# Steps of a weight transform called after two of three matmul groups of the output projection

## The chip, the cores and the metric

The kernel runs on one core of a Trainium2 chip. The metric is the device time of one launch in microseconds (us). TensorE (PE) multiplies and writes to PSUM; VectorE (DVE), ScalarE (ACT) and GpSimd (POOL) do the elementwise work, and POOL has no access to PSUM; SyncE (SP) issues all the transfers. Each engine takes its instructions from a queue of its own, in order.

## The reference

One layer of a decoder on 1024 prompt tokens and 8 x 4 sample tokens (1056 in all), model width 1024, feed-forward width 2816, in fp32:

```
m = mixer(x)                                   # HGRN2 heads and retention heads, gated and normalised
x = layer_norm(alpha * x + m @ w_out)          # "output projection", then the first norm
hidden = silu(x @ w_gate) * (x @ w_up)         # 22 blocks of 128 hidden features
x = layer_norm(alpha * x + hidden @ w_down)
```

It returns x and the states of the two kinds of heads.

## The kernel before

All activations are transposed: features on partitions, tokens on the free axis, in four quarters `q` of 264 tokens. Each fp32 factor is split into a high part (a cast on ACT, L214) and a low part (a subtraction on POOL or DVE, L215), and each product is three matmuls: high x high, high x low, low x high. A group of 8 factor blocks is thus 24 matmuls into one PSUM bank `pj`; there are four such banks.

The stages that matter here follow each other so. The **output projection**, `oproj(pr)` for `pr` = 0 and 1 (two quarters each): for each of 8 output blocks `m` and both quarters one group, 32 groups in all; L1112 adds the result to `Y` on DVE. Its weights come through `w_out(m)` as raw tiles `wr` and are split into `bh` and `bl` (L214 on ACT, L215 on POOL). Then the **first norm** of each quarter (`norm`): squares on ACT (L771) summed on DVE (L773), a column sum on TensorE (L756), `rstd` with three Newton steps on DVE (L761, L239 to L243), a matmul that spreads `rstd` over the tokens (L747), the scaling (L784 on DVE, L788 on ACT or L786 on DVE), and the split into `X`, whose low part is on POOL for six of eight blocks. Then the **plain products**, `gu`: for each quarter, gate and up of the hidden blocks 0 and 1, L250 from `X`, with L1004 on ACT and L1005 on DVE behind them. Then the **block products** (`unit`, L921), which compute the other 20 hidden blocks in pairs with seven products in place of eight; their weights are combined in `blocks` (L896 to L903 on POOL). At the end w_down is applied (L1166) in the same seven-product way.

For that last stage the combined blocks ("forms") of w_down are prepared early, by the generator `forms()`, and kept in DRAM (`wb`). It goes over the 11 pairs `p` of w_down's row blocks with three buffers in turn (tile `XC`, `p % 3`). Per pair: two loads of 512 KB (L1018); a row sum on DVE (L1033, the "reduce"); two operations on POOL (L1035, L1036) in the pair's first step; two more (L1040, L1041) in its second; and four stores of 256 KB (L1022). A load into a buffer waits until the stores from it have landed. All loads and stores are issued by SP, among the loads of weights (L223) and of `Y` (L1099) and the stores of hidden values (`hd`, L978).

```
        wf = forms()
            ...
            for p in range(3):
                load(p)
            yield
            for p in range(NPAIR):
                ...
                yield          # after store(p - 1), reduce, L1035, L1036
                ...
                yield          # after load(p + 2), L1040, L1041
            store(NPAIR - 1)
```

So `wf` has 24 steps: one for the first three pairs' loads, 22, and the last store. `next(wf, None)` takes one. Before, it stands in `oproj` behind each `m` (16 steps) and in the plain products behind each of 8 calls of `gu`. `combine(1)`, which needs the buffers' space, takes whatever is left. Other side work (the norms, `combine`, `total` with L800) is in a list of generators from which `tick` takes steps.

Where an instruction is written is not where it runs: the program is put in order per engine by a scheduler that works with its own estimates before the run. A step that is called sooner is thus placed sooner, and the rows around it are placed anew, on every engine.

Of the kernel before, what the change touches and what calls it, by code (L numbers as in the profile page):

```python
# [141 lines left out]
def body(tc, ctx, a):  # L142
# [11 lines left out]
    def pj():  # L154
        return psb["p"].tile([P, 512], F32, tag="pj", name="pj", bufs=psb["pj"])
# [89 lines left out]
    def group(out, ls, rs, rate):  # L245
        n = len(ls) * 3
        i = 0
        for (lh, ll), (rh, rl) in zip(ls, rs):
            for l, r in ((lh, rh), (lh, rl), (ll, rh)):
                PE.matmul(out, l, r, start=(i == 0), stop=(i == n - 1))  # L250
                i += 1
            if i == n // 2:
                tick(rate)
        tick(rate)

    def wk(w):
        return [(hi[:, k], lo[:, k]) for hi, lo in w for k in range(hi.shape[1])]

    def xk(c0, n):
        return [(X[:, 0, k, c0:c0 + n], X[:, 1, k, c0:c0 + n]) for k in range(KT)]  # L260


    with ExitStack() as ctxA:
# [450 lines left out]
        def w_out(m):  # L714
            wo[m] = load_w(wc[:, :, m * P:(m + 1) * P].rearrange("k p n -> p k n"))
# [6 lines left out]
    with ExitStack() as ctxB:  # L722
# [15 lines left out]
        def qs_(q):  # L738
            return slice(q * CQ, (q + 1) * CQ)
# [25 lines left out]
        def norm(q, g, b, w1=3, w2=3):  # L765
            n, sl = CQ, qs_(q)
            yield
            s2 = tt("s2")
            for m in range(KT):
                q2 = mx()[:, :n] if m else s2  # L770
                S.activation(q2, Y[:, m, sl], AF.Square)  # L771
                if m:
                    V.tensor_tensor(s2, s2, q2, op=add)  # L773
                if m % 2:
                    yield
            for _ in range(w1):
                yield
            rs = rstd([s2], n)
            for _ in range(w2):
                yield  # L780
            rb = spread(rs, n)
            for m in range(KT):
                y = Y[:, m, sl]
                V.tensor_tensor(y, y, rb, op=mul)  # L784
                if m in TA:
                    V.tensor_scalar(y, y, g[:, m:m + 1], b[:, m:m + 1], op0=mul, op1=add)  # L786
                else:
                    S.activation(y, y, AF.Identity, bias=b[:, m:m + 1], scale=g[:, m:m + 1])  # L788
                split(X[:, 0, m, sl], X[:, 1, m, sl], y, G if m in LG else V)
                if m % 2 and m < KT - 1:  # L790
                    yield
# [70 lines left out]
        def combine(pr):  # L862
            s0, s1 = qs_(2 * pr), qs_(2 * pr + 1)
            if pr:
                for _ in wf:
                    pass
                XB.append(pb.tile([P, 2, 3, HK, CQ], F32R, tag="XC", name="XC", bufs=1))
            yield
            for k in range(HK):
                t3, t2, t4 = [mx()[:, :CQ] for _ in range(3)]  # L870
                S.copy(t3, Y[:, HK + k, s1])
                V.tensor_tensor(t3, t3, Y[:, k, s1], op=sub)
                V.tensor_tensor(t2, t3, Y[:, k, s0], op=add)
                split(*btile("T3", pr, k), t3)
                yield
                V.tensor_tensor(t4, Y[:, HK + k, s0], t2, op=sub)
                split(*btile("T2", pr, k), t2)
                split(*btile("T4", pr, k), t4)
                yield
# [10 lines left out]
        def blocks(src, c, eng=None):  # L890
            E = eng or G
            w1, w2 = load_raw(src[c]), load_raw(src[c + 1])
            a11, a12, a21, a22 = w1[:, :HK], w1[:, HK:], w2[:, :HK], w2[:, HK:]
            out = {"A11": block(a11, eng)}
            f1 = pb.tile([P, HK, P], F32, tag="s1", name="s1", bufs=1)
            E.tensor_tensor(f1, a21, a22, op=add)  # L896
            E.tensor_tensor(a21, a11, a21, op=sub)
            E.tensor_tensor(a11, f1, a11, op=sub)  # L898
            out["S2"] = block(a11, eng)
            out["S3"] = block(a21, eng)  # L900
            out["S1"] = block(f1, eng)
            out["A12"] = block(a12, eng)
            E.tensor_tensor(a12, a12, a11, op=sub)  # L903
            out["A22"] = block(a22, eng)
            out["S4"] = block(a12, eng)
            return out
# [104 lines left out]
        def forms():  # L1011
            def raw(p):
                o = p % 3 * 2 * D
                return spare[:, o:o + 2 * D]

            def load(p):
                for i in range(2):
                    nc.sync.dma_start(raw(p)[:, i * D:i * D + D], a["w_down"][2 * p + i])  # L1018

            def store(p):  # L1020
                for n in range(4):
                    nc.sync.dma_start(wb[n, :, :, p, :].rearrange("m p n -> p m n"),  # L1022
                                      raw(p)[:, n * 512:n * 512 + 512].rearrange("p (m n) -> p m n", n=P))
# [5 lines that stand above are left out]
                a11, a21, a12, a22 = [raw(p)[:, n * 512:n * 512 + 512] for n in range(4)]  # L1029
                if p:  # L1030
                    store(p - 1)
                with behind(V):
                    V.tensor_reduce(rows[:, :2, p], raw(p).rearrange("p (i n) -> p i n", i=2), axis=AX, op=add)  # L1033
                with behind(G):
                    G.tensor_tensor(a11, a11, a21, op=sub)  # L1035
                    G.tensor_tensor(a21, a21, a22, op=add)  # L1036
                yield
                if p and p + 2 < NPAIR:
                    load(p + 2)
                G.tensor_tensor(a22, a22, a11, op=sub)  # L1040
                G.tensor_tensor(a12, a12, a22, op=sub)  # L1041
# [4 lines that stand above are left out]
# [47 lines left out]
                cnt["h"] += 1  # L1093
            return out

        cnt = {"w": 0, "h": 0}

        def xload(q, m):
            nc.sync.dma_start(Y[:, m, qs_(q)], xc[m, :, qs_(q)])  # L1099

        def oproj(pr):
            qs = (2 * pr, 2 * pr + 1)
            for i, m in enumerate(list(range(KT))[::1 - 2 * pr]):
                if m not in wo:
                    w_out(m)
                    wo.pop(m - 2 if pr == 0 else m + 2, None)
                for q in qs:
                    out = pj()[:, :CQ]
                    w, x = wk(wo[m]), xk(q * CQ, CQ)
                    group(out, [w[k] for k in GO], [x[k] for k in GO], RO)  # L1110
                    y = Y[:, m, qs_(q)]
                    V.scalar_tensor_tensor(y, y, ALPHA, out, op0=mul, op1=add)  # L1112
                    if pr == 0:
                        xload(q + 2, m)
                next(wf, None)
            for q in qs:
                side.append((("n1", q), norm(q, l1g, l1b)))
            side.append((("cb", pr), combine(pr)))
# [4 lines left out]
        for pr in range(2):  # L1123
            oproj(pr)

        h = {}
# [10 lines left out]
        for p in range(1, NPAIR):  # L1137
            h = {}
# [3 lines left out]
            w = blocks(a["w_gate"], 2 * p)  # L1142
# [91 lines left out]
def _program(ins):  # L1234
    import concourse.bacc as _bacc

    nc = _bacc.Bacc("TRN2", target_bir_lowering=False, num_devices=1, dynamic_dma_scratch_size=2048)
    a = {n: nc.dram_tensor(f"in_{n}", v.shape, mybir.dt.from_np(v.dtype), kind="ExternalInput").ap() for n, v in ins.items()}
    for n, s in _OUT.items():
        a["o_" + n] = nc.dram_tensor(f"out_{n}", s, F32, kind="ExternalOutput").ap()  # L1240
    a["st"] = [a["sh"], a["sr"]]
    a["so"] = [a["o_hp"], a["o_rp"]]
    a["sso"] = [a["o_hs"], a["o_rs"]]
    a["yT"] = a["o_yT"]
    with tile.TileContext(nc, schedule_with_timeline_sim=True) as tc, ExitStack() as ctx:
        body(tc, ctx, a)
    return nc
# [12 lines left out]
```

## Time and profile before

| | |
|---|---|
| time of the runs | 1316.63 us median of 3 (1314.59 to 1319.09) |
| profiled execution | 1313.48 us, span 1311.4 us |
| PE busy | 1285.0 us, 98% |
| DVE, ACT, POOL busy | 772.6, 506.9, 748.0 us |
| transfers | 170.50 MB, 130 GB/s over the span |
| output projection | from about 497 to 593 us |
| plain products | from about 593 to 648 us |
| block products, w_down | from 648 to 1060 us, to the end |

The times of all rows are from the start of the span. A row of an engine's timeline has the idle time ahead of it in brackets, and what ended it. "Busy" of PE counts matmuls that overlap, so that the number of matmuls in a stretch tells more than its busy time.

### The profile page before, as it was taken

How to read it: one execution, taken by the hardware profiler on the slowest of the kernel's cores; microseconds unless marked ns; L12 is line 12 of the kernel's file. 1: busy time of each engine (PE TensorE's matmuls, PEld its weight loads, DVE VectorE, ACT ScalarE, POOL GpSimd, SP SyncE). 2: the span in 40 equal slices, each digit the busy share in tenths (PEclk: the TensorE clock that was granted, in tenths of full speed). 3: DMA queues.
4: the chain of work that ended last, by engine and by line, in shares of the span. 5: the costliest groups of instructions: out<-in, count | busy, mean ns of one | idle time of the engine just before them, and what ended most of it. 6: DMA issues, size and time to landing. Idle time of an engine off the chain costs nothing.

```text
span 1311.4 us, 29620 instructions
## 1 busy us (share of the span) xinstructions
PE 1285.0 (98%) x11622; PEld 1259.1 (96%) x11622; DVE 772.6 (59%) x1675; ACT 506.9 (39%) x1120; POOL 748.0 (57%) x698
## 2 busy tenths in 40 slices
PE   9999999999999999999999999999999999999896
PEld 8999999999999999999899999999999999999896
DVE  7255443656575665489754654346544683777843
ACT  7243442232323233256542323323233354443552
POOL 2853331312122126798989888798786537675650
PEclk9999999999999999999999999999999999999898
DMA  8455312202111116987433323233232495656541
GB/s 287 141 174 187 134 35 83 69 16 80 55 65 52 50 51 212 300 244 237 138 94 102 123 91 102 75 102 119 94 103 70 145 304 163 180 180 180 156 135 67
DMA packets 156411, 170.50 MB, mean 130 GB/s; under 512 B 12272, under 2 KB 138864, under 8 KB 156272
## 3 DMA queue, kind: packets, MB, share of 16 engines
q1 hardware_dynamic: 156272, 168.62, 40.9%
q8 instruction: 91, 1.49, 0.5%
q14 instruction: 48, 0.39, 0.1%
HBM read 118.66 MB, written 49.91 MB: 129 GB/s over the span
## 4 chain that ended last, share of the span: by engine, by line
PE 91%; DVE 2%; POOL 2%; DMA 2%; issue 1%; ACT 1%; SPq 0%; ACTq 0%; POOLq 0%; DVEq 0%
PE pj L250 35%; PE mx L921 17%; PE pj L1166 16%; PE pj L921 14%; PE mx L482 1%; PE mx L625 1%; PE mx L595 1%; PE mx L627 1%; PE mx L250 1%; PE mx L577 1%; POOL X L215 1%; PE mx L666 1%; PE mx L537 1%; DMA XB<-hd 0%; DMA wr<-in_w_in 0%
## 5 line engine op out<-in xcount | busy, mean ns | idle before, releaser
L215 POOL TENSOR_TENSOR bl<-wr,bh 128x512 fp32r<-128x512 f32 x212 | 280.5, 1334 | 249.6 <-ACT bh L214 245.0
L250 PE MATMUL pj<-X,bh 128*128 128x352 f32 (+1 forms) x1888 | 417.9, 310 | 4.9 <-POOL X L215 3.3
L250 PEld LDWEIGHTS pj<-X,bh 128*128 128x128 f32 x1888 | 313.4, 189 | 9.6 <-POOL X L215 3.7
L250 PE MATMUL pj<-X,bl 128*128 128x352 f32 (+1 forms) x944 | 290.5, 308 | 0.1
L214 ACT CAST bh<-wr 128x512 fp32r<-128x512 f32 x220 | 133.0, 619 | 252.2 <-POOL wr L898 65.6
L250 PEld LDWEIGHTS pj<-X,bl 128*128 128x128 f32 x944 | 178.7, 189 | 0.8 <-DVE bl L215 0.4
L1166 PE MATMUL pj<-XC,X 128*128 128x264 f32 x858 | 149.1, 286 | 0.0
L1166 PE MATMUL pj<-XB,X 128*128 128x264 f32 x858 | 148.2, 285 | 0.0
L921 PE MATMUL pj<-X,bh 128*128 128x264 f32 x672 | 126.3, 287 | 0.4 <-DVE u L932 0.4
L1166 PEld LDWEIGHTS pj<-XC,X 128*128 128x128 f32 x858 | 123.1, 189 | 0.0
L1166 PEld LDWEIGHTS pj<-XB,X 128*128 128x128 f32 x858 | 122.6, 189 | 0.0
L921 PE MATMUL mx<-X,bh 128*128 128x264 f32 x608 | 112.4, 284 | 0.0
L921 PEld LDWEIGHTS pj<-X,bh 128*128 128x128 f32 x672 | 104.2, 188 | 0.9 <-DVE u L932 0.6
L1053 POOL TENSOR_TENSOR XC<-XC 128x264 fp32r<-128x264 f32 x71 | 67.0, 944 | 62.1 <-ACT XC L1052 62.0
L250 PE MATMUL pj<-bh,X 128*128 128x256 f32 x512 | 96.2, 285 | 0.0
L921 PE MATMUL pj<-X,bl 128*128 128x264 f32 x336 | 95.2, 284 | 0.0
L921 PEld LDWEIGHTS mx<-X,bh 128*128 128x128 f32 x608 | 93.8, 188 | 0.0
L1053 POOL TENSOR_TENSOR XB<-XB 128x264 fp32r<-128x264 f32 x71 | 68.9, 970 | 37.6 <-ACT XB L1052 32.6
L921 PE MATMUL mx<-X,bl 128*128 128x264 f32 x304 | 85.9, 282 | 0.0
L250 PEld LDWEIGHTS pj<-bh,X 128*128 128x128 f32 x512 | 79.9, 189 | 1.7 <-issue 1.0
L250 PE MATMUL pj<-bl,X 128*128 128x256 f32 x256 | 72.5, 283 | 0.0
L959 DVE TENSOR_TENSOR h<-mx,u 128x264 f32<-128x264 f32 x54 | 23.0, 431 | 69.0 <-PE mx L921 68.0
(260 smaller groups left out, 2659.2 us busy)
## 6 DMA issues: line engine op xcount, KB each, us to landing
hd<-h SPq DMA_DIRECT2D x154, 132.0 KB, 2.1
wr<-in_w_in SPq DMA_DIRECT2D x23, 512.0 KB, 3.7
XC<-in_w_down SPq DMA_DIRECT2D x22, 512.0 KB, 5.1
wb<-XC SPq DMA_DIRECT2D x44, 256.0 KB, 4.9
wr<-in_w_gate SPq DMA_DIRECT2D x22, 512.0 KB, 4.0
wr<-in_w_up SPq DMA_DIRECT2D x22, 512.0 KB, 3.6
XB<-hd SPq DMA_DIRECT2D x77, 132.0 KB, 3.2
XC<-hd SPq DMA_DIRECT2D x77, 132.0 KB, 3.4
```

The costliest lines, as they stand in the source:

```text
L214: S.copy(hi, src)
L215: (eng or V).tensor_tensor(lo, src, hi.bitcast(F32), op=sub)
L250: PE.matmul(out, l, r, start=(i == 0), stop=(i == n - 1))
L482: PE.matmul(into(B32 * b, (c % 4) * w), k[:, o:o + B32], cols(q, o), start=True, stop=True)
L537: PE.matmul(a_ps[:, c * C:(c + 1) * C], k[:, cc], q[:, cc], start=True, stop=True)
L577: PE.transpose(t_ps[:, c * C:(c + 1) * C], k[:, (4 * b + c) * C:(4 * b + c + 1) * C], ident)
L595: PE.matmul(d_ps[:, c * P:(c + 1) * P], tk[:, 4 * b + c], v[:, 4 * b + c], start=True, stop=True)
L625: PE.matmul(o[:, c * P:(c + 1) * P], at[:, cc], v[:, cc], start=True, stop=(cc == 0))
L921: PE.matmul(bank[pr], l[:, k], rs[k][r], start=(first and n == 0), stop=(n == 3 * HK - 1), skip_group_check=not first)
L959: V.tensor_tensor(g, ps, u, op=add)
L1053: eng.tensor_tensor(lo, raw, hi.bitcast(F32), op=sub)
L1166: PE.matmul(out, l, r, start=(i == 0), stop=(i == 3 * NPAIR - 1))
```

## The change

A counter of groups is kept in `cnt["g"]`, and `oproj` calls `next(wf, None)` inside the loop over the quarters, behind every group whose number is not a multiple of three: 22 calls in place of 16. The call behind each `gu` is not touched; it finds two steps left, where it found eight.

```
-        cnt = {"w": 0, "h": 0}
+        cnt = {"w": 0, "h": 0, "g": 0}
...
                     V.scalar_tensor_tensor(y, y, ALPHA, out, op0=mul, op1=add)
                     if pr == 0:
                         xload(q + 2, m)
-                next(wf, None)
+                    cnt["g"] += 1
+                    if cnt["g"] % 3:
+                        next(wf, None)
```

The scheduler's order moves with it (the changed file has two lines more, so lines from L1115 on are two higher there). First place: DVE, from the reduce that precedes quarter 2's `rstd`. `mx` is the tile with the variance, `XC` the buffers of the forms. Before (the reduce is pair 8's):

```order
L1005 TENSOR_TENSOR h<-pj,u 128x264
L1033 TENSOR_REDUCE rows<-XC 128x2
L761 TENSOR_SCALAR mx<-mx 128x3
L239 TENSOR_SCALAR ny_7641<-mx 128x3
L241 TENSOR_TENSOR mx<-mx,ny_7641 128x3
L242 SCALAR_TENSOR_TENSOR mx<-mx,ny_7641 128x3
```

Now (the reduces are those of pairs 9 and 10, and L1155 and L1156 are L1153 and L1154 of before):

```order
L1033 TENSOR_REDUCE rows<-XC 128x2
L773 TENSOR_TENSOR s_7587<-s_7587,mx 128x264 x2
L1033 TENSOR_REDUCE rows<-XC 128x2
L761 TENSOR_SCALAR mx<-mx 128x3
L1005 TENSOR_TENSOR h<-pj,u 128x264
L1155 TENSOR_SCALAR rows<-rows 128x22
L239 TENSOR_SCALAR ny_7670<-mx 128x3
L1156 TENSOR_TENSOR rows<-rows 128x11
L241 TENSOR_TENSOR mx<-mx,ny_7670 128x3
L242 SCALAR_TENSOR_TENSOR mx<-mx,ny_7670 128x3
L1005 TENSOR_TENSOR h<-pj,u 128x264
```

The last two reduces have moved from behind quarter 2's `rstd` to ahead of it. In the same way pair 5's reduce now stands ahead of quarter 0's L761, where pair 3's was the last before. On TensorE L747 of quarter 2 stands behind 1046 matmuls of 264 columns, before behind 1020.

Second place: POOL, from the first operation of `blocks` (L896) to the first X splits of quarter 2 (L215 with `X<-Y,X`). Before:

```order
L896 TENSOR_TENSOR s_8261<-wr 128x512
L1041 TENSOR_TENSOR XC<-XC 128x512
L1036 TENSOR_TENSOR XC<-XC 128x512
L897 TENSOR_TENSOR wr<-wr 128x512
L1040 TENSOR_TENSOR XC<-XC 128x512
L800 TENSOR_TENSOR s_8384<-Y 128x264
L1041 TENSOR_TENSOR XC<-XC 128x512
L800 TENSOR_TENSOR s_8384<-s_8384,Y 128x264 x6
L215 TENSOR_TENSOR X<-Y,X 128x264 x2
```

Now, the end of the same piece:

```order
L800 TENSOR_TENSOR s_8384<-s_8384,Y 128x264
L1040 TENSOR_TENSOR XC<-XC 128x512
L800 TENSOR_TENSOR s_8384<-s_8384,Y 128x264
L1041 TENSOR_TENSOR XC<-XC 128x512
L1035 TENSOR_TENSOR XC<-XC 128x512
L800 TENSOR_TENSOR s_8384<-s_8384,Y 128x264
L215 TENSOR_TENSOR X<-Y,X 128x264 x2
L1036 TENSOR_TENSOR XC<-XC 128x512
L800 TENSOR_TENSOR s_8384<-s_8384,Y 128x264
```

Counted over the queue since the output projection began, 32 operations of the forms stood ahead of these X splits before and 41 now, of `total` (L800) 7 before and 4 now; 12 of the forms stood behind them, now 3.

Third place: SP, from the first load of pair 9. Now:

```order
L1018 DMA XC<-in_w_down 128x1024
L223 DMA wr<-in_w_gate 128x1024
L1022 DMA wb<-XC 128x4x128
L1018 DMA XC<-in_w_down 128x1024
L1022 DMA wb<-XC 128x4x128 x2
L1018 DMA XC<-in_w_down 128x1024
L978 DMA hd<-h 128x264
L223 DMA wr<-in_w_gate 128x1024
L1022 DMA wb<-XC 128x4x128 x2
L1018 DMA XC<-in_w_down 128x1024
```

The loads (L1018) are pair 9's two and pair 10's two. Before, up to pair 9's second load:

```order
L223 DMA wr<-in_w_gate 128x1024
L1022 DMA wb<-XC 128x4x128
L223 DMA wr<-in_w_up 128x1024
L1022 DMA wb<-XC 128x4x128
L1018 DMA XC<-in_w_down 128x1024
L978 DMA hd<-h 128x264
L1022 DMA wb<-XC 128x4x128 x3
L1018 DMA XC<-in_w_down 128x1024
```

What moved is the weight load of `blocks` (the second L223 `in_w_gate`), from ahead of pair 9's first load to behind pair 10's first load.

## Rows read from the trace of the kernel before

**Rows 1.** The page's head: span, busy time by engine, TensorE's clock in tenths

```profile
span 1311.4 us, 29620 instructions
PE 1285.0 (98%) x11622; PEld 1259.1 (96%) x11622; DVE 772.6 (59%) x1675; ACT 506.9 (39%) x1120; POOL 748.0 (57%) x698
PEclk9999999999999999999999999999999999999898
```

**Rows 2.** Busy time by stretch, instructions in parentheses; then clock, DMA share, GB/s

```profile
506.00:560.00 54.00, 54.00 (x444) 53.84 (x444) 24.03 (x46) 13.18 (x28) 38.10 (x30) 1.00 1.00 309
560.00:600.00 40.00, 40.00 (x333) 40.00 (x332) 37.01 (x78) 26.66 (x64) 39.76 (x38) 1.00 0.76 226
600.00:610.00 10.00, 10.00 (x86) 10.00 (x84) 8.55 (x25) 4.49 (x14) 6.34 (x6) 1.00 0.95 299
610.00:620.00 10.00, 8.81 (x74) 8.60 (x72) 8.88 (x19) 7.63 (x20) 9.61 (x12) 1.00 0.83 258
630.00:640.00 10.00, 7.38 (x44) 6.74 (x43) 9.66 (x19) 6.81 (x18) 9.76 (x11) 0.83 0.50 145
```

**Rows 3.** What TensorE waited for, 560 to 860 us: total, times, longest

```profile
PE pj L250 <- POOL X L215: 3.3, 2, 2.1
PE pj L921 <- DVE u L932: 0.4, 1, 0.4
PE pj L250 <- DVE X L215: 0.3, 1, 0.3
PE pj L250 <- ACT X L214: 0.2, 1, 0.2
```

**Rows 4.** TensorE's timeline: start, us, then line, operation, count, idle time before

```profile
561.84 0.73 PE L747 MATMUL mx<-cst,rs 128*128 128x128 f32 x6
...
612.06 0.73 PE L747 MATMUL mx<-cst,rs 128*128 128x128 f32 x6
...
618.79 0.39 PE L250 MATMUL pj<-X,bh 128*128 128x264 f32 x1 [1.19 <-POOL X L215]
...
634.70 0.39 PE L250 MATMUL pj<-X,bh 128*128 128x264 f32 x1 [2.11 <-POOL X L215]
...
648.26 0.41 PE L921 MATMUL pj<-X,bh 128*128 128x264 f32 x2
```

**Rows 5.** POOL's timeline, same columns

```profile
551.16 1.30 POOL L1035 TENSOR_TENSOR XC<-XC 128x512 f32<-128x512 f32 x1 [4.01 <-DVE rows L1033]
...
592.41 2.55 POOL L215 TENSOR_TENSOR bl<-wr,bh 128x512 fp32r<-128x512 f32 x2
...
613.08 4.96 POOL L800 TENSOR_TENSOR s<-s,Y 128x264 f32<-128x264 f32 x6
617.99 1.47 POOL L215 TENSOR_TENSOR X<-Y,X 128x264 fp32r<-128x264 f32 x2
...
633.85 4.40 POOL L215 TENSOR_TENSOR X<-Y,X 128x264 fp32r<-128x264 f32 x6
```

**Rows 6.** What SP waited for, 500 to 660 us: total, times, longest

```profile
SPq L1018 <- DMA wb<-XC: 44.2, 11, 5.9
```

**Rows 7.** DVE's timeline: a reduce behind a load, then quarter 2's rstd

```profile
548.79 2.29 DVE L1033 TENSOR_REDUCE rows<-XC 128x2 f32<-128x2048 f32 x1 [5.11 <-DMA XC<-in_w_down]
...
606.93 0.16 DVE L761 TENSOR_SCALAR mx<-mx 128x3 f32<-128x3 f32 x1
609.01 0.42 DVE L773 TENSOR_TENSOR s<-s,mx 128x264 f32<-128x264 f32 x1
610.80 0.43 DVE L1005 TENSOR_TENSOR h<-pj,u 128x264 f32<-128x264 f32 x1 [1.37 <-PE pj L250]
...
641.14 0.17 DVE L1153 TENSOR_SCALAR rows<-rows 128x22 f32<-128x22 f32 x1
641.91 0.73 DVE L1154 TENSOR_TENSOR rows<-rows 128x11 f32<-128x11 f32 x1
```

**Rows 8.** SP's timeline: issues that follow each other

```profile
606.58 0.33 SPq L1018 DMA_DIRECT2D XC<-in_w_down  x1
607.00 0.38 SPq L978 DMA_DIRECT2D hd<-h  x1
```

**Rows 9.** Transfers issued in 600 to 620 us; landing times of all loads, all stores

```profile
wb<-XC SPq DMA_DIRECT2D x6, 256.0 KB, 4.6
XC<-in_w_down SPq DMA_DIRECT2D x3, 512.0 KB, 4.0
DMA to landing us min/median/max: 3.4/5.1/9.2
DMA to landing us min/median/max: 2.3/4.9/9.1
```

**Rows 10.** ACT's timeline: the cast of quarter 2's first X

```profile
614.83 0.40 ACT L214 CAST X<-Y 128x264 fp32r<-128x264 f32 x1
```

## The prediction

> **What bounds the kernel now.** I read the page's busy table and clock row first [rows 1]. TensorE is busy for 1285.0 of 1311.4 us and its clock is at its upper level, 2.4 GHz, nearly everywhere. So a gain can only come from a stretch in which TensorE loses time, and a loss from a new place where it has to wait.
>
> The table of stretches shows where that is [rows 2]. From 506 to 600 us (the output projection) TensorE has no idle time and issues 777 matmuls. From 600 on each 10 us should hold about 84; 610 to 620 holds 74, and 630 to 640 holds 44, with a granted clock of 0.83 (part of it at 1.2 GHz). In the same table POOL is busy 39.76 of 40 us from 560 to 600 and 9.6 us or more of 10 in four of the six stretches after it: there it is the full queue. The list of waits names the cause [rows 3]: `pj` waits for POOL's split of X twice, 3.3 us in all. The timeline places them: 1.19 us before 618.79, where quarter 2 of the plain products begins, and 2.11 us before 634.70 for quarter 3 [rows 4].
>
> The stretch thus loses 1.19 us at quarter 2; at quarter 3 it loses 2.11, 0.22 (ACT) and 0.29 (DVE) us of waits and, by the clock, (1 - 0.83) x 10 = 1.7 us. That is 5.5 us, the most that removing all of it could give.
>
> **The change part by part.** The forms need 24 calls of `next(wf)`: one for the first loads, two for each of the 11 pairs, one for the last store. Before, 16 came in the output projection. Now 22 of 32 groups make a call (every third none), so two remain, and the line beside the plain products, which is still there, takes them. Nothing is removed: 44 POOL operations, 11 reduces on DVE, 22 loads and 44 stores stay. What moves is their place in four queues, shown in the section on the change.
>
> *POOL.* Before quarter 2's first X split, POOL now runs 41 operations of the forms where it ran 32, and 4 additions of `total` (L800) where it ran 7; the 28 weight splits, the 12 earlier X splits and two of `blocks` are in both. A 128x512 operation takes 1.3 us in a row of its kind; an L800 4.96 / 6 = 0.83 us; an X split 4.40 / 6 = 0.73 us [rows 5]. That is 9 x 1.3 - 3 x 0.83 = 9.2 us more. Before, the split began at 617.99; with no idle time won back it begins at 627.2 and ends at about 628.0. POOL was idle for 54 - 38.10 = 15.9 us between 506 and 560 [rows 2], which could take up the extra work. But its gaps before the fourth pair are waits for loads (4.01 us before 551.16, behind the reduce), and the transfers were at a share of 1.00 there: they don't come sooner because steps are called sooner. On SP one more 256 KB store now stands ahead of that pair's second load, 0.85 us at 309 GB/s [rows 2], so I start the fourth pair at 552.0. I win back at most 2.3 us.
>
> *SP and DVE.* There are only three buffers. A pair's second load waits for the stores of the pair three before it, and this is SP's largest wait: 44.2 us in 11 times [rows 6]. A reduce then waits for the load, and everything on DVE waits behind it: before 548.79 DVE stood for 5.11 us in this way [rows 7]. There nobody needed DVE. Now the reduces of pairs 9 and 10 stand ahead of quarter 2's `rstd` (L761 and its Newton steps); before, only pair 8's did, and its load was there. The matmul that spreads `rstd` (L747) follows it, then the scaling, then the X splits; TensorE stands at L747 or, behind it, at the X split.
>
> The chain, from POOL's order: from pair 3's first operation to the last one of pair 6 there are 32 operations of 128x512 and 11 X splits, 32 x 1.3 + 11 x 0.73 = 49.6 us, ending at 601.6 if POOL doesn't idle. Then SP must see pair 6's last store land; issue pair 9's second load and two stores; wait for the second of these (pair 7's) before pair 10's first load; pass that, an `hd` store and a weight load; issue a store of pair 7, wait for it, and issue pair 10's second load. An issue takes about 0.45 us [rows 8]. In 600 to 620 us a store landed in 4.6 and a load in 4.0 us (medians); the shortest of all were 2.3 and 3.4 [rows 9]. With the medians: 601.6 + 4.6 + 0.9 + 4.6 + 1.4 + 4.6 + 4.0 = 621.7. The reduce takes 2.29, `rstd` 2.1 (606.93 to 609.01), two evictions of 0.43 and two operations on `rows` of 0.17 and 0.73 stand between [rows 7]: L747 can run at 627.9. From L747 (612.06) to the end of ACT's cast (614.83 + 0.40) and a POOL split of 0.73 it took 3.9 us [rows 4, 5, 10]: the first X is ready at 631.8. With the shortest landings it is 624.3.
>
> So two queues, worked out apart, give 628.0 (or 625.7 with idle time won back) and 624.3 to 631.8. **I take 628.0**, the sum that rests on POOL operations alone and lies in the middle of the other. By the order alone it can't be ready before 619.1: quarter 2's L747 now stands 26 matmuls later, 612.06 + 26 x 0.12 + 3.9 (0.12 us is 40.00 us for 333 matmuls [rows 2]).
>
> A rule of the Trainium skill speaks against so late a chain: "DMA: Bandwidth & Descriptors", section "Anatomy of one DMA", gives about 2.0 us fixed plus bytes at 436 GB/s, as an estimate 2.6 us for a store and 3.2 us for a load. If that chain alone decided, the first X would by it be ready at 625.0 and the change would cost 3.5 us, under the bound of 0.3%; the page measured the gpsimd path, and the medians here disagree with it, 4.6 and 4.0 us on a queue that is 83 to 95% busy.
>
> *From the first X of quarter 2 on.* Before, TensorE needed 648.26 - 618.79 = 29.5 us to the first block product (L921), of which 4.3 us are quarter 3's losses above; 25.1 us are left for 192 matmuls and quarter 3's small ones. After a wait of some 10 us the clock will fall as it did after the 2.11 us wait: 1.7 us. Quarter 3's X is no longer late: its six splits follow 10.8 us behind quarter 2's first (6 X, 3 forms, 3 L800) and end near 642, when TensorE still has work. The weight splits of the first block product follow them directly, since pair 10's operations are now ahead. So L921 starts at 628.0 + 25.1 + 1.7 = 654.8, not at 648.26: **6.5 us later**. After that TensorE was never without work for long (0.4 us behind `u` [rows 3]), so nothing gives it back.
>
> *Smaller edits.* The reduce of pair 5 now stands ahead of quarter 0's `rstd`. Its load follows pair 2's last store; with the same medians L747 of quarter 0, at 561.84 before [rows 4], may wait 0 to 5 us. This costs nothing here: TensorE then arrives later at a wait that POOL and DVE end, up to the 10 us of that wait. Without that cover it costs its full size. The four weight splits of the second gate and up weight, 592.41 to about 599 before [rows 5], come by the same sum at 602 to 610; the order of the matmuls was changed along with them, and the same cover holds.
>
> The profiled run took 1313.48 us (span 1311.4), 3.15 below the median of 1316.63. 1313.48 + 6.5 = 1320.0; against the median, 1323.1. The ends 624.3 and 631.8 give +2.8 and +10.3, or 1319.4 to 1326.9.
>
> **The rivals.** *No change.* The stores and loads land nearer to the shortest rows, or POOL's early idle time is filled after all, and the first X comes between 619.3 and 625.5: L921 moves by -3.9 us (619.3 + 25.1, no slow clock) to +4.0 us, 1312.7 to 1320.6. For it: POOL idled 15.9 us before 560, and the landing times fall when the queue is less full. Against it: pair 10 still has to pass two stores in order.
>
> *Faster.* The reduce of pair 10 ends by 611, the nine extra operations all find idle time, and quarter 2's X comes at its earliest, 619.1, quarter 3's without a wait: L921 at 619.1 + 25.1 = 644.2, 4.1 us sooner, 1312.6. This decides itself at one point, whether the nine operations find idle time. For it: POOL has nine operations of the forms fewer behind that split. Against it: the DMA share of 1.00 in the window in which they would have to be prepared.
>
> *Worse than I sum.* If the stall at pair 5 or the late weight splits also hold POOL back (its weight splits wait for buffers that TensorE frees), the 5 us add to the 6.5: 1328.
>
> *It does not do what it says.* Two calls stay beside the plain products, and in POOL's queue 10 operations of the forms (16 before) still follow the first of `blocks`, seven of them ahead of quarter 2's X. This is no separate time: it is in the sum above.
>
> **How the numbers follow.** A measurement of this kernel tells about 0.3%, 4 us, from no change. My forecast with its worse form holds 0.63; nearly all of its own range is beyond that bound. No change has 0.30, faster 0.07, because even the earliest X gains just about 4 us. The range leaves out the faster case, the lower end of no change and what lies beyond the worse form: 1314 to 1328.
>
> **What would show it.** In the new profile: DVE waiting for `XC<-in_w_down` at the reduces of pairs 9 and 10, between 605 and 622; TensorE idle for 8 to 12 us before quarter 2's X or at L747 near 616 to 628, then a stretch below full clock; no wait at quarter 3; L921 from about 655; no difference after it. I am wrong if TensorE has no wait over 3 us at quarter 2, or if L921 starts before 650.

## The result, and the profile after

The changed kernel takes 1327.53 us (median of 6 runs, 1325.85 to 1329.24) where the kernel before takes 1317.86 (6 runs, 1314.59 to 1321.71): a ratio of 1.0072, interval 1.0054 to 1.0089. It is **slower by 9.7 us**, more than twice the bound of 0.3%. The prediction's sum gave 1323.1 in a range of 1314 to 1328: the sign is right, the time lies at the upper end, and the loss is half as large again as the 6.5 us of the sum.

The profiled run of the changed kernel took 1329.24 us, 15.8 more than that of before (1313.48). That is more than the medians differ by, since the one lies 1.7 us over its median and the other 4.4 under. The rows below explain this pair of runs; of the 9.7 us between the medians they tell where it may go, not how it divides. The head of its page, to lay beside [rows 1]:

```profile
span 1327.5 us, 29637 instructions
PE 1290.7 (97%) x11622; PEld 1263.2 (95%) x11622; DVE 773.0 (58%) x1675; ACT 506.3 (38%) x1120; POOL 744.5 (56%) x698
PEclk9999999999999999989999999999999999999898
```

The work is the same, and there is one more slice with a lower clock, around 600 us. The table of stretches, with the columns of [rows 2]:

```profile
506.00:560.00 54.00, 53.11 (x437) 52.90 (x437) 21.04 (x31) 12.47 (x26) 36.52 (x30) 1.00 1.00 318
560.00:600.00 40.00, 36.40 (x273) 35.97 (x273) 32.32 (x63) 16.24 (x38) 37.50 (x35) 0.91 0.88 272
600.00:610.00 10.00, 7.38 (x59) 6.98 (x57) 9.79 (x25) 7.28 (x21) 8.68 (x9) 1.00 0.59 190
610.00:620.00 10.00, 7.80 (x51) 7.80 (x52) 8.22 (x18) 6.06 (x17) 4.03 (x4) 0.83 0.45 123
620.00:640.00 20.00, 15.99 (x119) 15.38 (x118) 14.24 (x35) 8.40 (x24) 17.57 (x19) 0.93 0.55 160
640.00:660.00 20.00, 18.75 (x152) 18.54 (x151) 18.70 (x50) 12.15 (x35) 13.21 (x14) 0.98 0.26 81
```

The count of matmuls is the thing to read. From 560 to 600, **inside the output projection**, it falls from 333 to 273: 60 x 0.12 = 7.2 us are lost where before lost nothing. From 600 to 620 it falls from 160 to 110, 6.0 us. So TensorE is 13 us behind at 620, before quarter 2 of the plain products is reached, and POOL, the full queue of before, has only 4.03 us of work in 610 to 620. TensorE's waits from 560 to 860 us (total, times, longest; [rows 3] before):

```profile
PE mx L747 <- DVE rs L243: 4.3, 2, 3.3
PE pj L250 <- ACT X L214: 3.6, 2, 2.0
PE pj L250 <- ACT u L1004: 3.2, 1, 3.2
PE pj L250 <- DVE X L215: 1.2, 1, 1.2
PE pj L250 <- DVE h L1005: 1.0, 1, 1.0
```

None ends on POOL any more. The timeline places them ([rows 4] before):

```profile
566.07 1.45 PE L747 MATMUL mx<-cst,rs 128*128 128x128 f32 x6 [3.27 <-DVE rs L243]
...
602.37 0.48 PE L250 MATMUL pj<-X,bh 128*128 128x264 f32 x2 [1.58 <-ACT X L214]
...
612.20 0.51 PE L250 MATMUL pj<-X,bh 128*128 128x264 f32 x2 [3.24 <-ACT u L1004]
...
631.44 0.81 PE L747 MATMUL mx<-cst,rs 128*128 128x128 f32 x6 [1.00 <-DVE rs L243]
635.59 0.64 PE L250 MATMUL pj<-X,bh 128*128 128x264 f32 x3 [2.03 <-ACT X L214]
...
637.21 0.67 PE L250 MATMUL pj<-X,bh 128*128 128x264 f32 x2 [0.98 <-DVE h L1005]
...
643.50 0.39 PE L250 MATMUL pj<-X,bh 128*128 128x264 f32 x1 [1.25 <-DVE X L215]
...
664.69 0.41 PE L921 MATMUL pj<-X,bh 128*128 128x264 f32 x2
```

The first wait is at quarter 0's `rstd` (566.07), the next two in the plain products of quarter 0, the last four in quarter 2's. The first block product (L921) starts at 664.69, 16.4 us later than in [rows 4]; the spans differ by 16.1, so what comes after it adds and gives back next to nothing. From 545 to 665 us TensorE's waits add up to 14.6 us, in before to 4.2. By the granted clock, (1 - clock) x stretch, the stretches from 560 to 660 lose 3.6 + 1.8 + 1.4 + 0.4 = 7.2 us, in before 1.8. The two differences, 10.4 and 5.4, come to 15.8.

What stands behind each wait shows in the chain of work that ended last (start, us, what):

```profile
551.45 6.17 DMA wb<-XC
557.70 3.47 DMA XC<-in_w_down
...
563.44 0.16 DVE mx L761
...
581.40 4.01 DMA wb<-XC
585.48 3.74 DMA XC<-in_w_down
589.34 2.29 DVE rows L1033
591.63 2.71 DVE Y L784 x8
594.35 0.34 DVE Y L1112
594.68 6.88 DVE Y L786
601.59 0.37 ACT X L214
...
611.76 0.39 ACT u L1004
...
613.90 0.34 DVE h L1005
...
615.17 6.19 DMA wb<-XC
621.38 3.63 DMA XC<-in_w_down
```

Three times the same sequence is on the path: a store of the forms lands, the load into its buffer follows, the DVE's reduce follows that, and a norm stands behind the reduce on the DVE. And between the second and the third there is something new: one `L786` (scale and shift of a 128x264 slice on the DVE, 0.41 to 1.45 us in before) that held the path for 6.88 us.

### The profile page after: what moved, and what is told of

It reads as the page before. It is cut to its first block, busy times and chain, and to the rows that moved or that the text cites. A ratio compares the mean times of both kernels' runs of the same rounds, so it can differ in the third digit from the quotient of the medians.

```text
span 1327.5 us, 29637 instructions
## 1 busy us (share of the span) xinstructions
PE 1290.7 (97%) x11622; PEld 1263.2 (95%) x11622; DVE 773.0 (58%) x1675; ACT 506.3 (38%) x1120; POOL 744.5 (56%) x698
## 4 chain that ended last, share of the span: by engine, by line
PE 85%; DMA 6%; DVE 5%; ACT 2%; SPq 1%; issue 1%; POOL 0%; ACTq 0%; DVEq 0%
PE pj L250 31%; PE mx L921 16%; PE pj L921 14%; PE pj L1168 14%; PE mx L482 1%; DMA wb<-XC 1%; PE mx L625 1%; PE mx L595 1%; PE mx L627 1%; DMA wr<-in_w_down 1%; PE mx L250 1%; DMA XC<-hd 1%; DMA XC<-in_w_down 1%; DVE Y L786 1%; DVE X L215 1%
## 5 line engine op out<-in xcount | busy, mean ns | idle before, releaser
L215 POOL TENSOR_TENSOR bl<-wr,bh 128x512 fp32r<-128x512 f32 x212 | 279.4, 1328 | 248.6 <-ACT bh L214 243.7
L921 PE MATMUL pj<-X,bh 128*128 128x264 f32 x672 | 126.3, 286 | 0.0
L921 PE MATMUL mx<-X,bh 128*128 128x264 f32 x608 | 112.4, 284 | 0.0
L921 PEld LDWEIGHTS pj<-X,bh 128*128 128x128 f32 x672 | 104.3, 188 | 0.3
L921 PE MATMUL pj<-X,bl 128*128 128x264 f32 x336 | 95.6, 284 | 0.0
L921 PEld LDWEIGHTS mx<-X,bh 128*128 128x128 f32 x608 | 93.8, 188 | 0.0
L921 PE MATMUL mx<-X,bl 128*128 128x264 f32 x304 | 85.9, 282 | 0.0
```

The lines of the kernel that those rows point to most:

```text
L215: (eng or V).tensor_tensor(lo, src, hi.bitcast(F32), op=sub)
L921: PE.matmul(bank[pr], l[:, k], rs[k][r], start=(first and n == 0), stop=(n == 3 * HK - 1), skip_group_check=not first)
```

## The experiments

Three theories were tried. **D**: the reduces, which wait for loads that wait for stores, stand ahead of the norms. **P**: POOL's longer row ahead of the X splits, as in the sum of the prediction. **T**: DVE instructions such as the long L786 are held up while POOL runs without a gap. Each time is the median of 10 runs (4 for before_no_sums and norm_op_form) and stands beside that of the kernel before on the same chip; times are compared by their distance from it. The changed kernel lies 9.7 us over it. Nearly every edit also lets the scheduler place the other rows anew, and so takes away more than one thing.

| kernel | us (median) | before, same chip | ratio (interval) |
|---|---|---|---|
| no_sums | 1315.88 | 1318.26 | 0.9984 (0.9966 to 1.0002) |
| before_no_sums | 1309.97 | 1318.26 | 0.9946 (0.9929 to 0.9962) |
| norm_op_form | 1327.02 | 1318.26 | 1.0074 (1.0050 to 1.0097) |
| before_norm_op_form | 1317.70 | 1318.26 | 1.0000 (0.9982 to 1.0017) |
| no_sums_form | 1317.62 | 1317.52 | 0.9992 (0.9975 to 1.0008) |
| no_loads | 1320.09 | 1317.52 | 1.0016 (0.9998 to 1.0034) |
| late_sums | 1322.01 | 1317.52 | 1.0035 (1.0016 to 1.0054) |
| before_late_sums | 1318.54 | 1317.52 | 1.0002 (0.9984 to 1.0019) |
| no_sums_act_scale | 1323.14 | 1317.86 | 1.0030 (1.0014 to 1.0047) |
| first_half | 1322.03 | 1317.86 | 1.0041 (1.0024 to 1.0058) |
| second_half | 1320.87 | 1317.86 | 1.0025 (1.0007 to 1.0043) |
| before_sums_on_act | 1314.79 | 1317.86 | 0.9981 (0.9966 to 0.9995) |

### Without the row sums, in both kernels

```diff
+        V.memset(rows[:, :2], 0.0)
...
-                with behind(V):
-                    V.tensor_reduce(rows[:, :2, p], raw(p).rearrange("p (i n) -> p i n", i=2), axis=AX, op=add)
```

> The changed kernel without the row sums of w_down (L1033, the DVE's reduce of each pair; the sums are set to zero, the differences on POOL, the loads and the stores stay). Theory D (the chain store - load - reduce - rstd): in the changed kernel the reduces of pairs 5, 8 and 10 stand on the DVE's queue ahead of the norms of quarters 0, 1 and 2 and wait for loads that wait for stores; without them those three stalls go: 1314 to 1319 us, and PE waits for no rs (L243) and no u (L1004) between 555 and 635. Theory P (POOL's longer row ahead of the splits of X decides): the POOL keeps its row, so 1325 to 1328 us. In between (1320 to 1324): the reduces are half of it, and the rest is POOL or the slow L786.

> The kernel before without the row sums (same edit, the sums are zero). It is the measure for no_sums: what the reduces cost where they were. In the trace of before no wait of PE ends on a reduce, so theory D says 1315 to 1318 us, at most 3 us under before; theory P says the same, since POOL is untouched. If it falls by as much as no_sums does (8 us or more), then leaving the sums out is a gain by itself, and no_sums tells nothing of the change.

The changed kernel falls to 2.4 us under before, into the range of theory D. But the control falls too, by 8.3: leaving the sums out is a gain by itself, which neither theory had, and by the words of the expectation no_sums alone then tells nothing. Only the difference belongs to the change: with the sums it costs 9.7 us, without them 1315.88 - 1309.97 = 5.9. So about 4 us of it go with the reduces and 6 don't, where each of the two distances is good to some 2 us.

Against theory P speaks POOL's timeline in no_sums. As in the changed kernel, 41 operations of the forms stand ahead of quarter 2's first X split (and two additions of `total`, 7 in before), and yet it begins where it began in before (617.99):

```profile
617.88 1.45 POOL L215 TENSOR_TENSOR X<-Y,X 128x264 fp32r<-128x264 f32 x2
```

POOL no longer waited for the reduces (pair 3's first operation at 538.42, in the changed kernel at 552.44), and its early idle time took up the nine operations. In that run they cost nothing by themselves.

Where no_sums still loses shows in the stretch from 620 to 640, first of no_sums, then of before_no_sums:

```profile
620.00:640.00 20.00, 17.20 (x120) 16.99 (x119) 18.16 (x42) 9.33 (x27) 13.06 (x16) 0.83 0.26 81
```

```profile
620.00:640.00 20.00, 19.55 (x161) 19.23 (x160) 17.96 (x42) 10.06 (x27) 18.55 (x18) 1.00 0.62 181
```

41 matmuls fewer, 4.9 us. TensorE's timeline and the DVE's, in no_sums, say why:

```profile
623.55 1.23 PE L756 MATMUL mx<-cst,s 128*128 128x1 f32 x5 [2.80 <-DVE s L773]
```

```profile
613.33 9.82 DVE L786 TENSOR_SCALAR Y<-Y,par 128x264 f32<-128x264 f32 x2
```

L786 again, now 9.82 us for two, and a clock of 0.83 after TensorE's wait behind it: 2.8 + 0.17 x 20 = 6.2 us. That is near the 5.9 and speaks for theory T, but doesn't prove it: the two profiled runs are only 2.9 us apart (1315.15 and 1312.24), and TensorE also waits 2.1 us for POOL's weight splits in no_sums.

### The form of L786

```diff
-                    V.tensor_scalar(y, y, g[:, m:m + 1], b[:, m:m + 1], op0=mul, op1=add)
+                    V.scalar_tensor_tensor(y, y, g[:, m:m + 1], b[:, m:m + 1].to_broadcast([P, n]), op0=mul, op1=add)
```

> The changed kernel with L786 (scale and shift of a norm on the DVE) written as scalar_tensor_tensor in place of tensor_scalar: same engine, same place in the order, same result. In the changed kernel one such instruction took 6.96 us (594.6 to 601.56) while POOL ran its forms and splits without a gap until 601.4; all the others took 0.4 to 1.5. Theory T: that form of instruction is held up while POOL is busy; the new form takes about 0.43 us as L1112's do, ACT's wait of 4.43 us for it at 601.6 goes, and the kernel comes to 1321 to 1325 us. Theory D: the 7 us lie in the shade of the waits for the loads before and behind: 1326 to 1328 us.

> The kernel before with the same edit of L786. Its eight instructions took 0.41 to 1.45 us, and PE's waits there end on POOL, so both theories: within 2 us of before (1316 to 1319 us). If it gains as much as norm_op_form does against the changed kernel, the slow form is no part of what the change costs.

> no_sums with the other form of L786 as well (the row sums are left out, zero). no_sums came to 1315.9 us and before_no_sums to 1310.0, so some 6 us of the change are left that the sums don't explain. In the trace of no_sums two L786 at 613.3 took 9.8 us while POOL ran from 596 to 623 without a gap, and PE waited 2.8 us behind them and lost clock. Theory T (what is left is L786 held up by POOL's closed row): 1309 to 1312 us, and no instruction of L786 over 2 us. Theory P (what is left is POOL's longer row itself, as the sum of the prediction has it): 1314 to 1317 us.

No gain in any of the three. In the profiled run of norm_op_form no L786 was held (2.0 us for two at 594.0). POOL's order up to quarter 2's X and the DVE's order are those of the changed kernel, and L921 starts at 658.88, 5.8 us sooner than there and 10.6 later than in before. So of the 16 us of the changed kernel's profiled run some 10 come without a held L786. But this was the shortest of its four runs (1323.77); the median didn't follow (1327.02). no_sums_form decides on the form: two L786 of the new form took 8.22 us there. The form isn't the cause. T's range for it is missed by 5.6 us, P's by 0.6.

### No loads behind the third pair

```diff
-                if p and p + 2 < NPAIR:
-                    load(p + 2)
```

> The changed kernel without the loads of pairs 3 to 10 (the sums, the differences and the stores run on what lies in the three buffers; the forms are of the wrong pairs). The reduces keep their place and their 2.29 us, and wait for no load. Theory D (the turn of a buffer, store - load - reduce, is what the norms wait for): 1314 to 1319 us, and no wait of PE for rs over 1 us. If the reduces cost by their own time on the DVE (8 more of 2.3 us ahead of the norms) or POOL by its row: 1323 to 1328 us. The DMA engines have 8 MB less to move, so something may come off for that too: PE's waits tell.

The wait for `rs` is gone and 2.6 of the 9.7 us over before are left; at 1320.09 us the time is still 1.1 above D's range. The profile shows, once more, a held L786, and behind it TensorE's longest wait:

```profile
565.63 10.70 DVE L786 TENSOR_SCALAR Y<-Y,par 128x264 f32<-128x264 f32 x1
```

```profile
579.59 1.44 PE L756 MATMUL mx<-cst,s 128*128 128x1 f32 x6 [7.04 <-DVE s L773]
```

Both theories thus have something to show here: where the loads don't stop POOL, POOL's row closes, and a DVE instruction waits for it. There was no control of this on the kernel before, so how much of the 7.1 us that came back the change itself owes to the loads stays open.

### The sums one pair later

```diff
                 if p:
                     store(p - 1)
-                with behind(V):
-                    V.tensor_reduce(rows[:, :2, p], raw(p).rearrange("p (i n) -> p i n", i=2), axis=AX, op=add)
+                    late(p - 1)
...
+            def late(p):
+                with behind(V):
+                    V.tensor_reduce(four[:, :, p], raw(p).rearrange("p (i n) -> p i n", i=4), axis=AX, op=add)
```

> The changed kernel with each pair's reduce taken one pair later, after POOL's four differences of its pair (four sums of 512 columns each, from which the same row sums follow at the end). Nothing is left out. POOL no longer waits for the DVE, and the DVE reads a pair that has long landed, but the next load into the buffer waits for the reduce as well as for the store. Theory D: 1316 to 1321 us, no wait of PE for rs over 1 us. Against it: if the reduce now waits for POOL (its L1041 one pair before) ahead of a norm, the stall is only moved: 1325 to 1330 us.

> The kernel before with the same later reduce. before_no_sums was 8 us under before, so the order reduce - differences costs something there too: by theory D POOL's rows start earlier and its X of quarters 2 and 3 are not late: 1309 to 1314 us. If leaving out the DVE's 25 us of reduces was the gain, and not their place: 1316 to 1319 us.

In both kernels the third and fourth sum are swapped in the four small instructions at the end that put them together, so the means taken off the forms are not the reference's; the instructions are the same in number and size. late_sums is 4.5 us over before, 5.2 less than the changed kernel, and 1 us above D's range. The wait for `rs` at quarter 0 is still there (2.6 us): its reduce now waits 5.5 us for POOL's last difference of the pair, so the stall was partly moved, as the other reading had it. before_late_sums gains nothing, so the place of the reduces isn't what before pays 8.3 us for. Whether it is the DVE's 25 us of them, the last experiment asks.

### L786 off the DVE

```diff
-TA = (2, 5)
+TA = ()
```

> no_sums (row sums left out, zero) with the norms' scale and shift all on ACT: no L786 on the DVE. The form made no difference in no_sums_form: two L786 at 617.2 took 8.2 us there too, while POOL was busy for all of 600 to 620. Theory T, in its second form: not the form of L786 but any DVE instruction that reads and writes SBUF alone in a stretch where POOL runs without a gap waits for a gap; the 6 us between no_sums (1315.9) and before_no_sums (1310.0) are that wait, 2.8 us of PE behind it and the low clock after it (0.83 in 620 to 640). Without L786: 1309 to 1312 us and a clock of 1.00 from 560 to 640. Theory P (POOL's row by itself): 1314 to 1318 us. If the next such DVE instruction (L215, X of two slices) waits in its place, the time stays and the trace shows it at L215.

Not faster: 5.3 us over before, where no_sums was 2.4 under. Both ranges are missed. The last sentence of the expectation named the place, an L215, but the time didn't stay, it grew. The DVE's and POOL's timelines:

```profile
584.13 20.41 DVE L215 TENSOR_TENSOR X<-Y,X 128x264 fp32r<-128x264 f32 x1 [1.39 <-ACT X L214]
604.46 0.42 DVE L1112 SCALAR_TENSOR_TENSOR Y<-Y,pj 128x264 f32<-128x264 f32 x1
```

```profile
583.96 1.28 POOL L1036 TENSOR_TENSOR XC<-XC 128x512 f32<-128x512 f32 x1
...
602.99 1.26 POOL L1036 TENSOR_TENSOR XC<-XC 128x512 f32<-128x512 f32 x1
608.12 1.28 POOL L215 TENSOR_TENSOR bl<-wr,bh 128x512 fp32r<-128x512 f32 x1 [3.88 <-ACT bh L214]
```

An L215 that takes 0.4 to 1.6 us elsewhere took 20.41. POOL ran 19 instructions without a gap from 583.96 to 604.25, and the L215 ended 0.3 us after the last of them. TensorE waited 11.7 us for the eviction queued behind it (L1112).

### One half of the change at a time

```diff
-                    if cnt["g"] % 3:
+                    if cnt["g"] % (2 if pr else 3):
```

is the first half; the second has `(3 if pr else 2)`.

> The change in the first half alone: two of three groups in quarters 0 and 1 (11 steps), one of two in quarters 2 and 3 (8 steps); the rest beside the plain products. Theory D: pairs 3 to 5 come as early as in the changed kernel, so pair 5's reduce stands ahead of the norm of quarter 0 and waits for its load: the first stall (5.9 us of the profiled run, with its clock) is all there, the one at quarter 2 not or less: 1321 to 1325 us, and PE's wait for rs at 562 to 567. If the price lies in the last steps, ahead of quarter 2 (the sum of the prediction): 1317 to 1319 us.

> The change in the second half alone: one of two groups in quarters 0 and 1 (8 steps), two of three in quarters 2 and 3 (11 steps). Theory D: no wait for rs at quarter 0; pairs 6 to 9 come close together, so a reduce or a late difference stands ahead of quarter 2's norm: 1319 to 1323 us, PE's loss between 600 and 640. By the sum of the prediction, POOL's three more differences and the chain of loads ahead of quarter 2: the same, up to 1323. If only both halves together bring it: 1316 to 1319 us.

Both halves cost, 4.2 and 3.0 us, 7.2 of the 9.7 together. The first shows the wait that D gives it (3.09 us for `rs` at 566.74) and has no held instruction. The second lies in D's range, but not for D's reason: TensorE loses before 600, not between 600 and 640 (278 matmuls from 560 to 600, 333 in before). Its largest wait is 4.34 us for the DVE's L1112 at 595.14, behind an L786 of 11.25 us. This profiled run was the longest of its ten, 5.6 us over their median, so the held L786 explains that run; that T is also what the second half's 3.0 us are isn't shown.

### The sums on ACT

```diff
-                with behind(V):
-                    V.tensor_reduce(rows[:, :2, p], raw(p).rearrange("p (i n) -> p i n", i=2), axis=AX, op=add)
...
+            def late(p):
+                dump = ut().bitcast(BF16)[:, :512]
+                with behind(S):
+                    for n in range(4):
+                        S.activation(dump, raw(p)[:, n * 512:n * 512 + 512], AF.Identity, accum_out=four[:, n, p:p + 1])
```

> The kernel before with the row sums taken by ACT (four activations with a running sum per pair, one pair later, after POOL's differences), none on the DVE; nothing is left out. In before the DVE is busy 37.0 of the 40 us from 560 to 600 and 19.4 of 20 from 620 to 640, ACT 26.7 and 8.8. If the DVE's 2.3 us per pair are what before pays 8 us for (before_no_sums), 1309 to 1314 us. If it is the place of the sums (ACT now waits for POOL ahead of the casts of X): 1316 to 1322 us. before_late_sums, with the sums at the same place but on the DVE, was no better than before.

1314.79 us, 3.1 under before: the fastest version here that computes everything, though by 0.2% only, less than the prediction's bound of 0.3%. It lies between the two ranges, and of the 8.3 us of before_no_sums it brings 3.1, so the DVE's 25 us of reduces are not the whole of them. The profiled run, the longest of its ten (1319.96), has a held L786 too (8.53 us at 581.57), and TensorE waits 3.7 us for the DVE's `s`.

## Why the prediction held, and where its working failed

**What was right.** The bound (TensorE, with POOL and the buffers' turn behind it), the sign, and three places: pair 3's first operation, put at 552.0, started at 552.44; quarter 3's X was no longer late; and from L921 on next to nothing was given back (16.4 us there, 16.1 at the end). From the first X on, the 25.1 us to L921 came out too: 635.59 + 25.1, 2.2 us of waits at 637.21 and 643.50, and some 1.8 us of slow clock give 664.7 (664.69 measured). From the reduce of pair 10 to L747 it is right to a tenth (6.2, 6.34 measured, 625.10 to 631.44).

**What was luck.** That the time lies in the range is owed to the width of the range. By its own signs the prediction was wrong: TensorE was to have a wait of over 3 us at quarter 2, and the longest there was 2.03 (1.00, 2.03, 0.98 and 1.25, 5.3 us in all, not 8 to 12). TensorE's two longest waits, 3.27 and 3.24 us, came before quarter 2, where the sum counts nothing. The first X came at 635.59 and not at 628.0.

**The step that failed: a wait counted as an issue.** In the chain SP had to "pass that, an `hd` store and a weight load", for which the sum has about 0.45 us each [rows 8]. SP's timeline:

```profile
599.25 0.45 SPq L1018 DMA_DIRECT2D XC<-in_w_down  x1
...
607.41 0.34 SPq L1018 DMA_DIRECT2D XC<-in_w_down  x1
614.27 0.33 SPq L978 DMA_DIRECT2D hd<-h  x1
...
621.38 0.34 SPq L1018 DMA_DIRECT2D XC<-in_w_down  x1
```

SP stood from 607.75 to 614.27, 6.5 us. In [rows 8] the same store went out at once; here it has to wait for the product `h` (L1005, done at 614.24), and all that stands behind it on SP waits too: the weight load of `blocks` (issued at 614.69), pair 7's last stores, pair 10's second load. That load was issued at 621.38, when by the sum it should have landed (621.7).

Both queues met this one wait. POOL's row came out nearly as summed, but it stood still once for long:

```profile
619.21 1.29 POOL L896 TENSOR_TENSOR s<-wr 128x512 f32<-128x512 f32 x1 [5.97 <-DMA wb<-XC]
...
635.62 1.56 POOL L215 TENSOR_TENSOR X<-Y,X 128x264 fp32r<-128x264 f32 x2 [2.37 <-ACT X L214]
```

The profile puts the 5.97 us down to a store. But L896 reads the weights whose load went out behind the `hd` store at 614.69, and that load, the only one of w_gate issued in 600 to 625, took 4.4 us, to 619.1. The row ended at 633.25; without the 5.97 us it ends at 627.3, where the prediction had 627.2. Then it waited 2.37 us more for the other queue, store - load - reduce - `rstd`, which came later still: 3.8 us behind its own upper end of 631.8.

**Why `h` was late.** Not for TensorE: it had done what it could by 608.96 and stood until 612.20 for `u`, and between 567.6 and 643.5 the chain has no piece of it. `h` waited for `u`, which ACT computed at 611.76 behind its casts, and ACT had stood 4.43 us, to 601.59, for the held **L786** (6.88 us of the chain, and nowhere in the sum). Ahead of that L786 stands the reduce at 589.34, waiting for its load. The L786 is not all of it: in norm_op_form's profile, where none was held, SP still stood for 5.0 us at the same store (605.63 to 610.58).

**Two errors that cancel.** The chain has a wait that isn't there. The load at 599.25, taken for pair 9's second, is pair 10's first: pair 9's second half goes into the place of pair 6's, whose last difference (the seventh L1041 in POOL's queue) hadn't begun:

```profile
603.49 1.59 POOL L1041 TENSOR_TENSOR XC<-XC 128x512 f32<-128x512 f32 x1
```

So pair 9's second load is the one at 607.41, and pair 10's first had passed it. The sum waits for one store too many (4.6 + 0.9 us) and counts 1.4 us of issues where 7.8 passed. With pair 6's end at 605.08 in place of 601.6, and stores of 2.3 and 6.2 us in place of 4.6, it comes out 3.3 us early (621.7, 625.0 measured).

**The last step of the chain.** To L747 (above) it held. The 3.9 us from there to the first X were 4.15 to ACT's cast, behind which TensorE started, and 5.0 with the POOL split that the 3.9 us include.

**"This costs nothing here."** The stall at quarter 0's `rstd` came (3.27 us, in the middle of 0 to 5). TensorE lost 13 us before quarter 2 and waited 5.3 there: what it had lost was taken off that wait, as the working has it, but the end of the wait had moved. Whether the stall itself cost anything in the changed kernel isn't shown. In first_half, where TensorE waited 0.84 us for quarter 2's `rs` and not for its X, the same stall had little cover.

**The clock.** The sum carried 1.7 us of slow clock over from quarter 3 to quarter 2, no more. The granted clock was 0.91 in 560 to 600 and 0.91, 0.93 and 0.98 in the three stretches of 20 us after that: 7.2 us below the upper level, against 1.8 in before (0.91 in 620 to 640 alone). Seven waits of 0.98 to 3.27 us lie among them, in before one of 1.19 and one of 2.11 and three under 0.4.

**The rule of the Trainium skill** that I weighed, "DMA: Bandwidth & Descriptors", section "Anatomy of one DMA": its estimates were 2.6 us for a store and 3.2 for a load. The loads on the path took 3.47, 3.74 and 3.63 us and nearly bear it out; of the stores one agrees (issued at 605.11, landed by 607.41), and 6.17, 4.01 and 6.19 us don't. The loss is not the 3.5 us that it gave.

**The rivals.** "Worse than I sum" named 1328 us and is nearest in time. Its premise, that quarter 0's stall adds to the later one, isn't shown, and its way, POOL's weight splits held up by TensorE's buffers, is not what happened: POOL had no idle time from 552.44 to 573.92, around that stall. "No change" had POOL's early idle time filled; in no_sums it was, but there POOL didn't have to wait for the reduces.

## What to carry to other kernels

When a chain of transfers is summed, each store passed on the same queue is also a wait for the engine that makes its data, and everything issued behind it waits along: here a weight load for POOL and a load for the DVE, so that two queues that looked apart were late together. Look up, for each such store, when its data will be ready in the new order, and which buffer each load goes into. Side work that is only called sooner need not arrive sooner when its buffers turn at the pace of the DMA queue; it arrives in front of something else. And look for single instructions that are ten times longer than their kind: they can cost although nobody waits for the engine next to them.

## What the runs showed of the hardware

I had not expected single DVE instructions of 7 to 20 us. Seven of the 14 profiles have one: 6.96 us (changed kernel), 9.50 (no_sums), 7.82 (no_sums_form), 10.70 (no_loads), 11.25 (second_half), 8.53 (before_sums_on_act) and 20.41 (no_sums_act_scale). Each has its operands in SBUF alone, each ran while POOL went from one instruction to the next without a gap, and each ended 0.15 to 0.3 us after POOL stopped. POOL stopped because it had to wait for a cast by ACT, and in each of the seven ACT itself had stood for the held instruction or for one behind it on the DVE. In the changed kernel (POOL, then ACT):

```profile
600.67 0.73 POOL L215 TENSOR_TENSOR X<-Y,X 128x264 fp32r<-128x264 f32 x1
602.72 0.80 POOL L215 TENSOR_TENSOR X<-Y,X 128x264 fp32r<-128x264 f32 x1 [1.32 <-ACT X L214]
```

```profile
601.59 1.05 ACT L214 CAST X<-Y 128x264 fp32r<-128x264 f32 x3 [4.43 <-DVE Y L786]
```

POOL's gap begins at 601.40, and L786, begun at 594.60, ended at 601.56. So in these profiles the wait lasted until POOL had used up the instructions that were ready and came to one that needed, through ACT, what the DVE was held from making. The reduces, whose one input is in SBUF, kept their 2.27 to 2.29 us throughout.

The Trainium skill, "SBUF — State Buffer", section "Who interferes with whom", says that a DVE instruction with two SBUF inputs, or in a mode with two ports, contends with GpSimd for a shared pair of ports, that the second to issue blocks until the first is through, and that `tensor_reduce` never contends. The traces agree on the reduces, and the held instructions are of the kinds it names, if L786 ran in such a mode, which no trace shows. They differ on the length: the L215 was not held for one POOL instruction but for 19. That the shared ports are the cause is argued from that page; no run here takes them away.

Open is why most such instructions get in between two of POOL's (L786 took at most 1.45 us in before, with POOL busy for 39.76 of 40 us), so that the wait falls in another place in every kernel; and whether that is also why executions of one kernel lie 10 us and more apart here (before: 1313.5 to 1325.6 in 31 runs on one chip). The profiles point that way: of the seven with a held instruction six are runs of 1.7 to 5.6 us over the median of their kernel (no_sums is 0.7 under); of the seven without, four are 1.8 to 4.4 us under and three 0.4 to 2.3 over. If so, a single profile tells little of what T costs in the median. It wasn't tried to take every DVE instruction of that kind out of the stretch.
